# Down projection of a decoder layer: block products over seven instead of eight for 24 of 44 K tiles, in written order

## The chip, the cores and the metric

The kernel runs on one core of a Trainium2 chip. The metric is the device time of one execution in microseconds; the time shown for a kernel is the median of its runs. The profile is one further execution, taken with the hardware profiler on. The work uses TensorE (matmuls into PSUM), VectorE and ScalarE (elementwise), GpSimd (here mostly as the issuer of accumulating DMAs) and SyncE (the issuer of the other DMAs).

## What is computed

One post-norm layer with 512 tokens and width 2048. The change touches only the last stage, `ffn = act @ w_down`, and the residual that is added to it:

```
mix = jnp.einsum('bsm,md->bsd', jnp.concatenate([rg_out, at_out], axis=-1), w_out[i])
x = _layernorm(DEEPNORM_ALPHA * x + mix, ln_mix_g[i], ln_mix_b[i])           # x1
hu = _causal_dwconv(jnp.einsum('bsd,df->bsf', x, w_up[i]), ffn_conv_w[i], ffn_conv_b[i])
g, u = jnp.split(hu, 2, axis=-1)
ffn = jnp.einsum('bsf,fd->bsd', jax.nn.gelu(g) * u, w_down[i])                # 512 x 5632 @ 5632 x 2048
x = _layernorm(DEEPNORM_ALPHA * x + ffn, ln_ffn_g[i], ln_ffn_b[i])
```

All data is float32. The hidden width is 5632 = 44 tiles of 128; the output is 4 token tiles of 128 by 4 column blocks of 512.

## The kernel before, in words

**Numbers in two parts.** Every float32 operand of a matmul is split into a high part (a ScalarE copy to float32r, L113) and a low part (a VectorE subtraction, L114). `split` (L109) does both. A product is three matmuls, high times high, high times low and low times high (`mm3`, L117): each loads a 128x128 block of one operand and streams 512 columns of the other.

**The stages.** Input projections, the recurrent and attention heads, the output projection and its norm come first. Then the up projection: four hidden tiles are made plainly, and the other 40 by `class Pair` (L797 to L909). A pair makes the gate and the up tile of one hidden tile as one 2x2x2 block product with seven products, in the order of `PRODUCTS` (L70). The weight sums that this needs are made by accumulating DMAs that GpSimd issues (`onto`, L807) and by VectorE (L830, L841); each of the seven weights is then split whole, 128x1024 (L816), two steps ahead of its product. The pairs are written out by hand in steps (`step`, L914), one product a step, under `tc.manual_schedule()` (L965): there every engine and every DMA queue executes in written order. The activation of each pair is stored to a DRAM buffer `hidd` (L909).

**The down projection** (L978 to L1014) stands outside the manual schedule, so the scheduler of the language orders it. It goes in chunks of 12, 12, 16 and 4 K tiles (`CHUNKS`, L29). For each of the first three chunks and each column block, four PSUM banks (one for each token tile) take the products of all K tiles of the chunk, and VectorE adds the banks to `acc` (L1007). `acc` is made in the first chunk: x1 without its gain is loaded from the DRAM buffer `x1d` into it (L991), and two VectorE operations apply gain, shift and the residual factor ALPHA (L992, L993). The weights come through `Weights` (L157): six raw buffers of 128x1024 (`RAW_UP`, L54), three pairs of split buffers (`W_BUFS`, L55). The hidden tiles are loaded back and split by `ready` (L958).

**The last chunk** (L1018 to L1036) goes token tile by token tile, with weights that were split beforehand (`keep`), and each token tile is normalized and stored while the next is multiplied. It is the same in both kernels.

Buffers that the change shares: 56 tiles of 128x512 (`A_BUFS`), 12 temporary ones (`T_BUFS`), 8 PSUM banks.

Of the kernel before, what the change touches and what calls it, by code (L numbers as in the profile page):

```python
# [74 lines left out]
def f32(ap):  # L75
    return ap.bitcast(F32)
# [3 lines left out]
def trunk_kernel(  # L80
    ctx, tc, xT, x_tok, w_qkg, w_v, gate_w, w_out, w_up0, w_up, w_down, ln1, ln2, consts, out
):
    nc = tc.nc
# [119 lines left out]
    W = Weights()  # L203
# [717 lines left out]
    j = 0  # L921
# [21 lines left out]
        activate(i, pss)  # L943


    CH = CHUNKS[-1]
    wsrc = iter([w_down[n] for n in range(2 * FT)])
    for c, n in enumerate(CHUNKS[:-1]):
        for u in range(NF * n // 2):
            W.push([next(wsrc)])  # L950

    wlast = [(w, True) for w in wsrc]
    for u in range(len(wlast)):
        W.srcs.insert(len(W.srcs) - 2 * u, wlast[-1 - u])
    keep, gb = [], [[], []]
    hid = {}

    def ready(upto):  # L958
        for i in range(len(hid), min(upto, FT)):
            t = t_tile(F32, "hid")  # L960
            nc.sync.dma_start(t, hidd[i])
            hid[i] = split(t)

    last = NP * len(pairs)
    with tc.manual_schedule():  # L965
        for k in range(last):
            step(k, "early", 1, 8)
            step(k, "late", 7, 16)
            step(k, "before", -6, 5)
            step(k, "product", 0, NP)  # L970
            ready({last - 5: 4, last - 3: 12, last - 2: 16}.get(k, 0))
            if k == last - 4:
                W.load()
    for k in range(last, last + 9):
        step(k, "early", 1, 8)
        step(k, "late", 7, 16)

    acc = {}  # L978
    at = 0
    for c, n in enumerate(CHUNKS[:-1]):  # L980
        ready(at + n)
        for fb in range(NF):
            ps = [bank() for _ in range(QB)]
            if c == 0:

                g1, b1 = [t_tile(F32, "gb1") for _ in range(2)]
                for z, row in ((g1, ln1[0]), (b1, ln1[1])):
                    nc.sync.dma_start(z, row[fb * S : (fb + 1) * S].partition_broadcast(P))
# [5 lines left out]
            for u in range(n // 2):  # L994
                parts = W.take()
                for i in range(2):
                    kk = 2 * u + i
                    for tt in range(QB):
                        hs = [z[:, tt * P : (tt + 1) * P] for z in hid[at + kk]]
                        mm3(ps[tt], hs, parts[i], kk == 0, kk == n - 1)  # L1000
                    if fb == NF - 1 and kk:
                        ready(at + n + kk)
                if c == len(CHUNKS) - 2 and fb == NF - 1 and u >= n // 2 - len(wlast):
                    keep.append(W.take())
            for tt in range(QB):
                y = acc[tt, fb]
                nc.vector.tensor_tensor(y, y, ps[tt], ALU.add)  # L1007
            if c == len(CHUNKS) - 2 and fb < 2:
                for b in range(NF):
                    gb[fb].append(t_tile(F32, "gb"))  # L1010
                    nc.sync.dma_start(
                        gb[fb][b], ln2[fb, b * S : (b + 1) * S].partition_broadcast(P)
                    )
        at += n  # L1014


    ready(FT)
    for tt in range(QB):  # L1018
        tok = slice(tt * P, (tt + 1) * P)
        ns = RowNorm()  # L1020
# [23 lines left out]
def _layout(inputs):  # L1044
# [42 lines left out]
    a["w_down"] = rows(g["w_down"][0], CHUNKS)  # L1087
# [42 lines left out]
```

## Time and profile before

| | |
|---|---|
| median of 3 runs | 2056.37 us (2056.30 to 2056.94) |
| the profiled execution | 2058.12 us, its span in the trace 2055.9 us |
| TensorE busy (matmul) | 2040.5 us, 99% of the span |
| VectorE, ScalarE busy | 1369.0 us (67%), 1039.2 us (51%) |
| GpSimd busy | 108.8 us (5%) |
| pairs of the up projection | about 785 us to 1574 us |
| down projection, last chunk included | from 1562.7 us to the end |

A busy share is over the whole span; the stages differ, so the stage that the change touches is read by itself. A matmul's recorded duration (0.39 us) is not its cost, since matmuls are pipelined: the distance from one start to the next is. The same holds, more weakly, for VectorE and ScalarE, whose consecutive instructions overlap by some hundredths of a microsecond. "Step" means one product's time on TensorE.

### The profile page before, as it was taken

The page shows a single profiled execution, that of the slowest core. Times are in us where ns is not written, and L with a number is a line of the kernel's source. Part 1 is how long each engine was busy: PE and PEld are TensorE (multiplying, and loading weights), DVE is VectorE, ACT ScalarE, POOL GpSimd, SP SyncE. Part 2 cuts the span into 40 slices and gives each one's busy share as a digit, 9 for nine tenths or more (in the row PEclk, how much of TensorE's full clock was granted, in tenths as well). Part 3 has the DMA queues.
Part 4 walks back from the last instruction along what each step waited for, and adds up shares of the span by engine and source line. Part 5 has one row for each costly group of instructions (what it writes and reads, how often), then busy time and mean ns, then how long its engine had stood idle before and what let it go on. Part 6 is the DMA issues. An engine that isn't in the chain of part 4 may idle for free.

```text
span 2055.9 us, 27746 instructions
## 1 busy us (share of the span) xinstructions
PE 2040.5 (99%) x10535; PEld 1747.2 (85%) x10535; DVE 1369.0 (67%) x2148; ACT 1039.2 (51%) x1652; POOL 108.8 (5%) x161
## 2 busy tenths in 40 slices
PE   9999999999999999999999999999999999999997
PEld 7888888888888999888888888888888888888886
DVE  6566645767334677888888888888889643333346
ACT  4475735667223865656556556566565232222232
POOL 1000000010000100100100000001000000000000
PEclk9999999999999999999999999999999999999999
DMA  6322222222533434667667667666678743242322
GB/s 222 98 72 94 77 92 88 88 82 97 175 108 113 154 96 130 176 163 193 171 165 188 173 171 180 169 184 172 168 193 273 264 145 112 93 143 93 113 82 82
DMA packets 93156, 290.52 MB, mean 141 GB/s; under 512 B 10336, under 2 KB 10336, under 8 KB 93024
## 3 DMA queue, kind: packets, MB, share of 16 engines
q1 hardware_dynamic: 81504, 246.81, 35.9%
q0 software_dynamic: 11520, 41.95, 12.1%
q8 instruction: 83, 1.36, 0.3%
q14 instruction: 49, 0.40, 0.1%
HBM read 268.80 MB, written 19.92 MB: 140 GB/s over the span
## 4 chain that ended last, share of the span: by engine, by line
PE 94%; ACT 3%; DVE 1%; issue 0%; DMA 0%; SPq 0%; DVEq 0%
PE ps L120 55%; PE ps L134 37%; PE ps L364 1%; ACT gt L473 0%; PE ps L365 0%; ACT s L376 0%; PE ps L394 0%; PE ps L672 0%; ACT a L479 0%; DMA hid<-hidd 0%; ACT L491 0%; ACT L479 0%; ACT L473 0%; ACT L376 0%; DVE hh L495 0%
## 5 line engine op out<-in xcount | busy, mean ns | idle before, releaser
L114 DVE TENSOR_TENSOR wlo<-raw,whi 128x512 fp32r<-128x512 f32 (+1 forms) x672 | 599.4, 910 | 421.1 <-ACT whi L113 419.8
L113 ACT ACTIVATE whi<-raw 128x512 fp32r<-128x512 f32 (+1 forms) x672 | 523.0, 802 | 470.7 <-PE ps L120 415.4
L120 PE MATMUL ps<-wlo,hi 128*128 128x512 f32 x992 | 386.9, 390 | 0.6 <-DVE wlo L114 0.6
L120 PE MATMUL ps<-whi,hi 128*128 128x512 f32 x992 | 386.6, 390 | 0.6 <-ACT hi L113 0.6
L120 PE MATMUL ps<-whi,lo 128*128 128x512 f32 x992 | 386.5, 390 | 0.0
L134 PE MATMUL ps<-hl,whi 128*128 128x512 f32 x1280 | 320.5, 392 | 0.0
L134 PEld LDWEIGHTS ps<-hl,whi 128*128 128x128 f32 x1280 | 230.2, 189 | 41.1
L134 PE MATMUL ps<-x,whi 128*128 128x512 f32 x960 | 237.1, 389 | 0.0
L120 PEld LDWEIGHTS ps<-whi,hi 128*128 128x128 f32 x992 | 186.7, 188 | 40.3 <-ACT hi L113 1.3
L120 PEld LDWEIGHTS ps<-wlo,hi 128*128 128x128 f32 x992 | 186.7, 188 | 39.7 <-DVE wlo L114 1.0
L120 PEld LDWEIGHTS ps<-whi,lo 128*128 128x128 f32 x992 | 186.7, 188 | 38.6
L134 PEld LDWEIGHTS ps<-x,whi 128*128 128x128 f32 x960 | 180.2, 188 | 37.3
L120 PE MATMUL ps<-hi,whi 128*128 128x512 f32 x512 | 201.9, 394 | 0.0
L120 PE MATMUL ps<-hi,wlo 128*128 128x512 f32 x512 | 200.5, 392 | 1.1 <-DVE wlo L114 1.1
L120 PE MATMUL ps<-lo,whi 128*128 128x512 f32 x512 | 199.9, 390 | 0.0
L134 PE MATMUL ps<-hl,wlo 128*128 128x256 f32 x1280 | 172.9, 283 | 0.0
L134 PEld LDWEIGHTS ps<-hl,wlo 128*128 128x128 f32 x1280 | 164.6, 192 | 3.5 <-ACT cu L881 0.4
L134 PEld LDWEIGHTS ps<-x,wlo 128*128 128x128 f32 x960 | 131.0, 190 | 9.3
L134 PE MATMUL ps<-x,wlo 128*128 128x256 f32 x960 | 133.9, 282 | 0.0
L120 PEld LDWEIGHTS ps<-hi,wlo 128*128 128x128 f32 x512 | 96.1, 188 | 22.7 <-DVE wlo L114 2.4
L120 PEld LDWEIGHTS ps<-lo,whi 128*128 128x128 f32 x512 | 96.3, 188 | 18.5
L120 PEld LDWEIGHTS ps<-hi,whi 128*128 128x128 f32 x512 | 96.2, 188 | 18.3
(187 smaller groups left out, 2231.2 us busy)
## 6 DMA issues: line engine op xcount, KB each, us to landing
raw<-in_w_up SPq DMA_DIRECT2D x176, 512.0 KB, 5.1
raw<-in_w_down SPq DMA_DIRECT2D x88, 512.0 KB, 3.6
raw<-in_w_up POOLq DMA_DIRECT2D x80, 512.0 KB, 6.6
raw<-in_w_qkg SPq DMA_DIRECT2D x64, 512.0 KB, 3.6
raw<-in_w_out SPq DMA_DIRECT2D x32, 512.0 KB, 3.6
hidd<-cv SPq DMA_DIRECT2D x44, 256.0 KB, 3.9
hid<-hidd SPq DMA_DIRECT2D x44, 256.0 KB, 5.2
raw<-in_w_v SPq DMA_DIRECT2D x15, 512.0 KB, 4.4
```

The costliest lines, as they stand in the source:

```text
L113: nc.scalar.activation(hi, src, AF.Copy)
L114: nc.vector.tensor_tensor(lo, src, f32(hi), ALU.subtract)
L120: nc.tensor.matmul(ps, a, b, start=first and n == 0, stop=last and n == 2, skip_group_check=onto)
L134: nc.tensor.matmul(o, a, b, start=not onto and k == 0, stop=k == len(steps) - 1, skip_group_check=onto)
L364: nc.tensor.matmul(ps[:, :L], qs, k[c][:, :L], start=True, stop=False)
```

## The change

The down projection is written out in steps under the manual schedule, with the pairs. `plan` collects actions for a step, and `run` issues them in the order loads, adds from the banks, weight splits (`CUT`), other VectorE and ScalarE work (`SUM`), matmuls.

- The first chunk is 4 K tiles, done plainly (`end_chunk`, 16 steps); the last is 4 as before.
- Between them stand three chunks of 12 K tiles. Eight of the twelve go through block products: tokens in two halves, K in two groups of four, columns in two blocks (`j` and `2 + j`). For each chunk there are two such blocks (`mixed_block`, 22 steps each). A block has seven products instead of eight; the other four K tiles of the chunk are multiplied plainly, half of them straight into the banks of the block products (`plain_lo`), half into banks of their own (`plain_hi`).
- The sums of weights: two accumulating DMAs for each half of the K group (`onto`), two VectorE additions (`s2`, `s4`).
- The sums of hidden blocks (`hid_forms`): three splits of 256 columns, four VectorE additions or subtractions and four more splits for each of four pairs of hidden tiles. Those of the first chunk are made beside `end_chunk`, those of the next chunk beside the second block of the chunk before.
- The residual of x1 is made in place in `x1d` beside the pairs: load, scale (step residue 5 of a pair), shift (7 steps later), store (2 steps after that), 16 tiles, one for every two pairs. `acc` is then only loaded.
- The host lays `w_down` out by column block and pair of K tiles.

```diff
-CHUNKS = [12, 12, 16, 4]
+ENDS = 4
+MIXED, PAIRS, REST = 3, 4, 4
...
+    LOAD, ADD, CUT, SUM, PE = range(5)
...
+    def run(k):
+        for _, fn, args in sorted(todo.pop(k, []), key=lambda z: z[0]):
+            fn(*args)
...
+    def end_chunk(at, k0):
...
+        for fb in range(NF):
+            for u in range(ENDS // 2):
+                k = k0 + 4 * fb + 2 * u
+                plan(max(k - 8, k0 - 6 + 2 * fb + u), LOAD, weights, z, (fb, u), fb, at + 2 * u)
+                plan(k - 2, CUT, cut, w, (fb, u), z, (fb, u))
+                plan(k, PE, product, fb, u)
...
+    def mixed_block(at, j, k0):
...
+        def onto(name, g, n, u):
+            nc.gpsimd.dma_start(
+                z[name, u], w_down[2 * g + j, (at + n * PAIRS) // 2 + u], accum_op=ALU.add
+            )
+        def s2(u):
+            z["s2", u] = W.raw()
+            nc.vector.tensor_tensor(z["s2", u], z["s1", u], z["r11", u], ALU.add)
+        def s4(u):
+            nc.vector.tensor_tensor(z["s2", u], z["s2", u], z["r12", u], ALU.add)
+        def product(name, u):
+            to, new = {"p1": ("x", 1), "p5": ("y", 1), "p2": ("z", 1), "p3": ("y", 0)}.get(name, ("x", 0))
...
+            for i in range(2):
+                f = sides(form2[name, at + 2 * u + i])
+                for t in range(2):
+                    hs = [q[:, t * P : (t + 1) * P] for q in f]
+                    mm3(b[to][t], hs, parts(i), bool(new) and u + i == 0, u + i == 2, not new)
...
+        for u in range(2):
+            for k, fn, args in (
+                (-8, raw, ("s1", 1, 0, u)), (-8, onto, ("s1", 1, 1, u)), (-6, raw, ("r11", 0, 0, u)),
+                (0 + u, onto, ("r11", 1, 0, u)), (1, raw, ("r12", 0, 1, u)),
+                (8, raw, ("r22", 1, 1, u)),
+            ):
+                plan(k0 + k + u, LOAD, fn, *args)
+            plan(k0 + 6 + u, LOAD, weights, z, ("q1", u), lo, rest + 2 * u)
+            plan(k0 + 10 + u, LOAD, weights, z, ("q2", u), hi, rest + 2 * u)
+            for k, name, src in (
+                (-2, "p1", "r11"), (0, "p5", "s1"), (2, "p6", "s2"), (4, "p2", "r12"), (6, "p7", "r11"),
+                (8, "p3", "s2"), (14, "p4", "r22"), (16, "q2", "q2"),
+            ):
+                plan(k0 + k + u, CUT, cut, w, (name, u), z, (src, u))
+            plan(k0 + 10 + 2 * u, CUT, cut, w, ("q1", u), z, ("q1", u))
+            plan(k0 - 1 + 2 * u, SUM, s2, u)
+            plan(k0 + 5 + 2 * u, SUM, s4, u)
+            for k, name in zip((0, 2, 4, 6, 8, 10, 16), PRODUCTS):
+                plan(k0 + k + u, PE, product, name, u)
+            plan(k0 + 12 + 2 * u, PE, plain_lo, u)
+            plan(k0 + 18 + u, PE, plain_hi, "c", ta, u)
+            plan(k0 + 20 + u, PE, plain_hi, "d", tb, u)
+        for k, bank_, tts, fb, op in (
+            (2, "x", ta, lo, ALU.add), (4, "y", tb, hi, ALU.subtract), (6, "x", tb, lo, ALU.add),
+            (10, "x", tb, hi, ALU.subtract), (16, "z", ta, lo, ALU.add), (16, "y", tb, lo, ALU.add),
+            (18, "x", ta, hi, ALU.subtract), (20, "c", ta, hi, ALU.add), (22, "d", tb, hi, ALU.add),
+        ):
+            plan(k0 + k, ADD, added, bank_, tts, fb, op)
...
+    for n in range(QB * NF):
+        k = NP * (2 + 2 * n) + 5 - last
+        plan(k - 5, LOAD, load_z, zs, n)
+        plan(k, SUM, scale_z, zs, n)
+        plan(k + NP, SUM, shift_z, zs, n)
+        plan(k + NP + 2, LOAD, store_z, zs, n)
...
+        for k in range(last, last + END + 1):
+            step(k, "early", 1, 8)
+            step(k, "late", 7, 16)
+            run(k - last)
...
-                for tt in range(QB):
-                    y = acc[tt, fb] = a_tile(F32, "acc")
-                    nc.sync.dma_start(y, x1d[tt][:, fb * S : (fb + 1) * S])
-                    nc.vector.scalar_tensor_tensor(y, y, ALPHA, g1, ALU.mult, ALU.mult)
-                    nc.vector.scalar_tensor_tensor(y, b1, ALPHA, y, ALU.mult, ALU.add)
```

## Rows read from the trace of the kernel before

**Rows 1.** The page, parts 1 and 2: busy time by engine, granted clock by slice.
```profile
PE 2040.5 (99%) x10535; PEld 1747.2 (85%) x10535; DVE 1369.0 (67%) x2148; ACT 1039.2 (51%) x1652; POOL 108.8 (5%) x161
...
PEclk9999999999999999999999999999999999999999
```

**Rows 2.** The page, part 4: the chain that ended last, by line.
```profile
PE ps L120 55%; PE ps L134 37%; PE ps L364 1%; ACT gt L473 0%; PE ps L365 0%; ACT s L376 0%; PE ps L394 0%; PE ps L672 0%; ACT a L479 0%; DMA hid<-hidd 0%; ACT L491 0%; ACT L479 0%; ACT L473 0%; ACT L376 0%; DVE hh L495 0%
```

**Rows 3.** The chain in order of time, from 1540 us: start, length, what.
```profile
1574.05 471.53 PE ps L120 x2080
...
2045.61 0.69 DVE acc L585
```

**Rows 4.** Timeline of TensorE where the pairs end: start, length, line, count.
```profile
1562.69 1.09 PE L120 MATMUL ps<-whi,hi 128*128 128x512 f32 x4
1564.38 0.50 PE L120 MATMUL ps<-wlo,hi 128*128 128x512 f32 x1 [0.60 <-DVE wlo L114]
```

**Rows 5.** Stretches: length; busy PE, PEld, DVE, ACT, POOL (instructions); PEclk, DMA, GB/s.
```profile
1100.00:1200.00 100.00, 100.00 (x576) 88.30 (x576) 86.23 (x98) 60.40 (x78) 8.63 (x10) 1.00 0.68 178
...
1750.00:1800.00 50.00, 50.00 (x222) 41.40 (x222) 17.75 (x27) 11.03 (x19) 0.00 (x0) 1.00 0.31 101
```

**Rows 6.** Waits of all engines, 800 to 1550 us: total, times, longest.
```profile
DVE wlo L114 <- ACT whi L113: 87.1, 116, 2.6
...
ACT whi L113 <- PE ps L134: 10.3, 38, 0.3
```

**Rows 7.** Timeline of TensorE in the pairs, two places.
```profile
1314.84 2.00 PE L134 MATMUL ps<-hl,whi 128*128 128x512 f32 x8
...
1544.16 2.00 PE L134 MATMUL ps<-hl,whi 128*128 128x512 f32 x8
1546.00 1.98 PE L134 MATMUL ps<-x,whi 128*128 128x512 f32 x8
1547.81 1.11 PE L134 MATMUL ps<-x,wlo 128*128 128x256 f32 x8
1548.76 2.00 PE L134 MATMUL ps<-hl,whi 128*128 128x512 f32 x8
```

**Rows 8.** Timeline of VectorE in the pairs.
```profile
1309.43 1.22 DVE L830 TENSOR_TENSOR raw<-raw 128x1024 f32<-128x1024 f32 x1
1310.57 0.68 DVE L883 TENSOR_TENSOR cg<-cg,ps 128x512 f32<-128x512 f32 x1
1311.17 0.68 DVE L884 TENSOR_TENSOR cu<-cu,p 128x512 f32<-128x512 f32 x1
1311.77 1.22 DVE L114 TENSOR_TENSOR wlo<-raw,whi 128x1024 fp32r<-128x1024 f32 x1
```

**Rows 9.** Timeline of VectorE, 256-column work ahead of the pairs.
```profile
772.31 0.42 DVE L762 TENSOR_TENSOR t<-t,x1f 128x256 f32<-128x256 f32 x1
772.65 0.42 DVE L761 TENSOR_TENSOR t<-x1f 128x256 f32<-128x256 f32 x1
```

**Rows 10.** Weight splits on ScalarE by form, whole span: busy, mean ns.
```profile
L113 ACT ACTIVATE whi<-raw 128x1024 fp32r<-128x1024 f32 x280 | 294.6, 1052 | 15.2 <-PE ps L134 10.3 <-PE ps L120 4.2 <-DMA raw<-in_w_up 0.4
```

**Rows 11.** DMA issues, 800 to 1550 us: count, KB each, median us to landing.
```profile
raw<-in_w_up SPq DMA_DIRECT2D x151, 512.0 KB, 5.2
raw<-in_w_up POOLq DMA_DIRECT2D x77, 512.0 KB, 6.0
```

**Rows 12.** The accumulating DMAs of L810, 800 to 1550 us: time to landing.
```profile
DMA to landing us min/median/max: 5.5/6.0/9.9
```

**Rows 13.** Timeline of VectorE as the down projection begins.
```profile
1581.38 0.68 DVE L993 SCALAR_TENSOR_TENSOR acc<-gb,acc 128x512 f32<-128x512 f32 x1
1581.98 1.28 DVE L992 SCALAR_TENSOR_TENSOR acc<-acc,gb 128x512 f32<-128x512 f32 x2
```

**Rows 14.** Waits of SyncE's DMA queue, 800 to 1550 us: total, times, longest.
```profile
SPq L909 <- DVE cv L907: 337.1, 38, 8.9
```

**Rows 15.** Timeline of SyncE's DMA issues in the pairs.
```profile
1313.62 0.33 SPq L909 DMA_DIRECT2D hidd<-cv  x1
```

More of the change, by code (lines that the diff above doesn't have):

```diff
@@ L943, in trunk_kernel @@
         activate(i, pss)
[L946 to L954, printed above, removed]
-    keep, gb = [], [[], []]
[L956 to L962, printed above, removed]
@@ new lines, in split_hid, with add_to, adds, plain @@
+    def split_hid(z, i):
+        hid[i] = split(z.pop(i))
+    def add_to(y, ps, op):
+        nc.vector.tensor_tensor(y, y, ps, op)
+    def adds(k, tts, fb, pss, op=ALU.add):
+        for n, tt in enumerate(tts):
+            plan(k, ADD, lambda tt=tt, n=n: add_to(acc[tt, fb], pss[n], op))
+    def plain(pss, tts, parts, at, first, last, onto=False):
+        for i in range(2):
+            for n, tt in enumerate(tts):
+                hs = [z[:, tt * P : (tt + 1) * P] for z in hid[at + i]]
+                mm3(pss[n], hs, parts(i), first and i == 0, last and i == 1, onto)
@@ new lines, in cut, with side_by, product @@
+    def cut(w, name, z, src):
+        w[name] = split(z[src], *W.pair())
+    def side_by(w, name):
+        return lambda i: [z[:, i * S : (i + 1) * S] for z in w[name]]
+    def end_chunk(at, k0):
+        z, w, pss = {}, {}, {}
+        def product(fb, u):
+            if u == 0:
+                pss[fb] = [bank() for _ in range(QB)]
+                for tt in range(QB):
+                    adds(k0 + 4 * fb + 4, [tt], fb, pss[fb][tt : tt + 1])
+            plain(pss[fb], range(QB), side_by(w, (fb, u)), at + 2 * u, u == 0, u == ENDS // 2 - 1)
+        for fb in range(NF):
[4 more added lines that the diff above has]
+                plan(k, PE, product, fb, u)
@@ new lines, in plan_forms, with raw, added, plain_lo @@
+    def plan_forms(at, ks):
+        for p in range(PAIRS):
+            load, *stages = hid_forms(at, p)
+            plan(ks[p][0] - 5, LOAD, load)
+            for k, fn in zip(ks[p], stages):
+                plan(k, SUM, fn)
+    BLOCK = 22
+    def mixed_block(at, j, k0):
+        z, w, b = {}, {}, {}
+        lo, hi = j, 2 + j
+        ta, tb = (0, 1), (2, 3)
+        rest = at + 2 * PAIRS
+        def raw(name, g, n, u):
+            weights(z, (name, u), 2 * g + j, at + n * PAIRS + 2 * u)
+        def onto(name, g, n, u):
[9 more added lines that the diff above has]
+            to, new = {"p1": ("x", 1), "p5": ("y", 1), "p2": ("z", 1), "p3": ("y", 0)}.get(name, ("x", 0))
+            if new and u == 0:
+                b[to] = [bank(), bank()]
+            parts = side_by(w, (name, u))
+            for i in range(2):
+                f = sides(form2[name, at + 2 * u + i])
+                for t in range(2):
+                    hs = [q[:, t * P : (t + 1) * P] for q in f]
+                    mm3(b[to][t], hs, parts(i), bool(new) and u + i == 0, u + i == 2, not new)
+        def added(bank_, tts, fb, op):
+            for n, tt in enumerate(tts):
+                add_to(acc[tt, fb], b[bank_][n], op)
+        def plain_lo(u):
+            plain(b["z"] + b["y"], ta + tb, side_by(w, ("q1", u)), rest + 2 * u, False, u == 1, True)
+        def plain_hi(name, tts, u):
+            if u == 0:
+                b[name] = [bank(), bank()]
+            plain(b[name], tts, side_by(w, ("q2", u)), rest + 2 * u, u == 0, u == 1)
+        for u in range(2):
[26 more added lines that the diff above has]
+            plan(k0 + k, ADD, added, bank_, tts, fb, op)
@@ new lines, in trunk_kernel, with load_acc @@
+    raws = {}
+    for i in range(ENDS):
+        plan(-9 + i // 2, LOAD, load_hid, raws, i)
+        plan(-5 + i // 2, CUT, split_hid, raws, i)
+    def load_acc(fb):
+        for tt in range(QB):
+            acc[tt, fb] = a_tile(F32, "acc")
+            nc.sync.dma_start(acc[tt, fb], x1d[tt][:, fb * S : (fb + 1) * S])
+    for fb in range(NF):
+        plan(-3 + fb, LOAD, load_acc, fb)
+    end_chunk(0, 0)
+    START = 4 * NF
+    plan_forms(ENDS, [[1, 2, 3], [5, 6, 7], [9, 10, 11], [12, 13, 14]])
@@ new lines, in trunk_kernel, with load_gb, split_keep @@
+    END = k1 + BLOCK
+    def load_gb(n, fb):
+        gb[n].append(t_tile(F32, "gb"))
+        nc.sync.dma_start(gb[n][fb], ln2[n, fb * S : (fb + 1) * S].partition_broadcast(P))
+    def split_keep(z, n):
+        keep.append([split(z[n][:, i * S : (i + 1) * S]) for i in range(2)])
+    for n in range(2):
+        for fb in range(NF):
+            plan(k1 + 2 + 2 * fb + n, LOAD, load_gb, n, fb)
+    kept = {}
+    for n, (k, kl) in enumerate(((11, 8), (13, 9), (15, 12), (17, 13), (19, 14), (20, 15), (22, 16), (22, 17))):
+        plan(k1 + kl, LOAD, weights, kept, n, n // 2, FT - ENDS + 2 * (n % 2))
+        plan(k1 + k, SUM, split_keep, kept, n)
@@ new lines, in trunk_kernel, with load_z @@
+    for n, k in enumerate((12, 14, 18, 19)):
+        plan(k1 + k - 4, LOAD, load_hid, raws, FT - ENDS + n)
+        plan(k1 + k, SUM, split_hid, raws, FT - ENDS + n)
+    last = NP * len(pairs)
+    def load_z(z, n):
+        fb, tt = divmod(n, QB)
+        if tt == 0:
+            z["g"], z["b"] = [t_tile(F32, "gb1") for _ in range(2)]
+            for m, row in ((z["g"], ln1[0]), (z["b"], ln1[1])):
+                nc.sync.dma_start(m, row[fb * S : (fb + 1) * S].partition_broadcast(P))
+        z[n] = t_tile(F32, "z")
+        nc.sync.dma_start(z[n], x1d[tt][:, fb * S : (fb + 1) * S])
@@ L970, in trunk_kernel @@
             step(k, "product", 0, NP)
[L971 to L988, printed above, removed]
-                for tt in range(QB):
-                    y = acc[tt, fb] = a_tile(F32, "acc")
-                    nc.sync.dma_start(y, x1d[tt][:, fb * S : (fb + 1) * S])
-                    nc.vector.scalar_tensor_tensor(y, y, ALPHA, g1, ALU.mult, ALU.mult)
-                    nc.vector.scalar_tensor_tensor(y, b1, ALPHA, y, ALU.mult, ALU.add)
[L994 to L1017, printed above, removed]
+            run(k - last)
+        for k in range(last, last + END + 1):
+            step(k, "early", 1, 8)
+            step(k, "late", 7, 16)
+            run(k - last)
+    at = FT - ENDS
     for tt in range(QB):
```

65 lines of the change are left out of this document (64 added, 1 removed).

## The prediction

> **What bounds the kernel now.** I read the busy shares first: TensorE is busy 99% of the span at full granted clock in every slice [rows 1]. A busy share alone proves little where matmuls are pipelined, so the chain that ended last comes next: 55% and 37% of the span are TensorE at the two matmul helpers (L120, L134), and no other entry is above 1% [rows 2]. Then the stage of the change: from 1574.05 us on, 2080 matmuls take 471.53 us in one unbroken piece [rows 3]; that is 0.2267 us each, end to end, at granted clock 1.00 [rows 5]. So the down projection is paid by the matmul, and in that stretch VectorE is busy 17.75 of 50 us and ScalarE 11.03. After the last matmul there are 10.3 us of norm and store (2045.61 to 2055.9) [rows 3], which both kernels have.
>
> The model for the changed stage is the pairs, which already work as the changed stage will: seven products, splits two steps ahead, written order. There TensorE is busy 100.00 of 100 us beside a VectorE that is busy 86.23 [rows 5], and among the waits there is none of TensorE; what they hold of the splits is VectorE waiting for ScalarE's copies and ScalarE waiting for TensorE to give back a split buffer [rows 6].
>
> **What is removed.** One product of a block goes over four K tiles (two weight buffers of two) and two token tiles, three matmuls each: 4 x 2 x 3 = 24 matmuls of 512 columns. Eight become seven, in 3 chunks x 2 blocks = 6 blocks: 6 x 24 = 144 matmuls less, 2112 to 1968. At 0.2267 us this is **32.6 us**. The pitch of the new products could differ, since their stationary blocks come from tiles with both parts side by side. The nearest row is the pairs: eight 512-column matmuls take 1546.00 - 1544.16 = 1.84 us (0.230) or 1547.81 - 1546.00 = 1.81 us (0.226) [rows 7]. For the 6 x 7 x 24 = 1008 matmuls of the products that bounds the pitch's part at -1 to +3 us; I take 0, as the shapes are those of L120.
>
> **The seam between pairs and down projection.** Four matmuls start at 1562.69 and the fifth only at 1564.38, after VectorE's low part [rows 4]: 1564.38 - (1562.69 + 4 x 0.2267) = 0.8 us lost. In the changed kernel the first product's weights are split two steps ahead and its hidden tiles four to five steps ahead, so this could go. But new seams come (pairs to plain chunk, plain chunk to blocks, block to block), so I take 0 gain, bounds -0.8 to +3 us.
>
> **What is added on VectorE.** Prices are start-to-start: 1.14 us for 1024 columns (1309.43 to 1310.57), 0.60 for 512 [rows 8], 0.34 for 256 [rows 9]. A step of the down projection is 12 matmuls, 2.72 us; a block is 22 steps, 59.9 us.
> - A block: 18 weight splits and 4 weight sums of 1024, 18 bank additions of 512: 22 x 1.14 + 18 x 0.60 = 36 us. With the four plain hidden tiles of the chunk 38 us, 64%.
> - A block beside which the next chunk's hidden sums are made (two such): 44 operations of 256 columns more, 36 + 44 x 0.34 = 51 us, 85%.
> - The plain chunk, 16 steps or 43.6 us: nine weight splits and one sum in it, 12 bank additions, 44 operations of 256, the end of the last pair (eight operations of 512): 10 x 1.14 + 20 x 0.60 + 44 x 0.34 = 38.4 us, 88%.
>
> No stretch is above what the pairs show beside an unbroken TensorE. Step by step, with 2.72 us of VectorE per step and what is left over carried on, the backlog is highest at the steps with four bank additions: 1.5 us in the chunk's fifth step, 1.8 in its thirteenth, 0.8 in step 16 of each block; it is gone two or three steps later each time. A weight split is written two steps, 5.44 us, ahead of its product. At a four-addition step the way to its end is: the last matmul's end 0.4, four additions 2.4, the low part 1.14, together 3.9 us (4.6 in the fifth step, where a convolution stands ahead). So it lies beside other work: cost 0. Should that cover fail, what is queued behind the waiting addition is the weight split, and TensorE waits for it; this is the first rival.
>
> ScalarE gets the same splits at 1.05 us [rows 10]; with half of that for a copy of 256, surely too much, 18 x 1.05 + 28 x 0.53 = 34 of 59.9 us in the fullest block. Off the path.
>
> **What is added in DMA.** A block issues 12 plain loads of 512 KB from SyncE and 4 accumulating ones from GpSimd in 59.9 us; three pairs (58 us) issue 12 and 6 and a few stores. So the queues see no more than they do now. Landing is 5.2 and 6.0 us [rows 11], 9.9 at worst for the accumulating ones [rows 12]. The shortest way is `r12`: its buffer is given back by the split of `p5` in the step before, it is cut three steps later (8.2 us): 3 us of cover beyond 5.2, and its product is two steps behind. The accumulation onto `r11` may start after the sums of steps -1 and 1 and is cut at 6 and 7, five steps or 13.6 us. Cost 0.
>
> Here a rule speaks against the change. The rows show that an accumulating 512 KB DMA from GpSimd lands in a median of 6.0 us and a plain one from SyncE in 5.2 us, while VectorE is busy 86% of the time [rows 5, 11]. The Trainium skill, page "SBUF — State Buffer", section "SBUF: two separate sides", says that a DMA from the GpSimd queue gets its descriptors written over a port that VectorE can hold in some modes, so that it looks blocked by VectorE; its section "Who interferes with whom" excepts two-input operations from that in part. By the rule the accumulations would land late and the sum would lose what the third rival says; by the rows they lose 0.8 us that is covered.
>
> **What is moved.** Residual: 32 VectorE operations of 512 columns (0.60 each [rows 13], 19 us) leave the down projection's start and go beside the pairs, one for each pair, with 16 loads, 16 stores (new: 4 MB) and 8 broadcast loads on SyncE's queue. A pair is seven steps of some 2.77 us (1548.76 - 1546.00 [rows 7]), 19.4 us; VectorE's busy time in it goes from 16.7 to 17.3 us. In the written order the operation stands behind the residue-5 split and sum and ahead of the two additions of the next step and the split of `p5`. That split ends at 1311.77 + 1.22 = 1312.99 [rows 8], and its product starts at 1314.84 [rows 7], with its low part used half a product later. 0.6 us more is covered by 1.85. On SyncE's queue the store and the next load stand just ahead of the `hidd` store, at which the queue waits up to 8.9 us for VectorE, 337 us in 38 waits [rows 14]; the store waits for a shift that VectorE does two steps before the product that `hidd` waits for. So they fall into that wait: cost 0. If the cover went, `r21`, the next load, would be late; that is the slower rival. What the down projection's start gains from the removal is nothing on TensorE's path.
>
> **Sum.** Span 2055.9 - 32.6 = 2023.3 us. The median of the runs stands 0.5 us above the span of the profiled execution (2056.37 to 2055.9; its own time is 2058.12), so 2023.7: forecast **2024 us**, 1.6% less.
>
> **Rivals.**
> - *VectorE paces the four-addition steps.* There are ten: four for the plain chunk, six in the blocks. If none of the backlog is hidden, each costs 0.8 to 1.8 us: 8 to 18 us, 2032 to 2042. For: VectorE is in the written order and stands waiting for banks with splits behind it. Against: the pairs, 86% busy, without a wait. Chance 0.15.
> - *Smaller pauses* at seams and a 0.230 pitch, up to +5 us: inside the forecast's own range.
> - *The accumulating DMAs come late.* It decides from a landing above 13.6 us, against 6.0 now and 9.9 at worst. At 20 us each block would lose some 5 us, 6 x 5 = 30: 2054, no change. Chance 0.03.
> - *It doesn't do what it says:* the seven products give no fewer TensorE cycles, because each matmul of the block costs 8/7 (0.259 us). The rows for 512 columns go from 0.226 to 0.230 [rows 7]. That would be 2056. Chance 0.01.
> - *Slower: the pairs get longer.* Place: the queue of SyncE and VectorE in each of 40 pairs. If scaling waits for its load or the `z` store holds up `r21`, the split of `p5` is late and TensorE waits in every other pair or more. It decides from 32.6 / 40 = 0.82 us per pair: then the gain is eaten. With nothing hidden, VectorE's 0.60 us and one DMA issue of 0.33 us [rows 15] per pair make 40 x 0.93 = 37 us: 2061. Against it: 1.85 us of cover on VectorE, up to 8.9 us on the queue. Chance 0.05.
>
> **How the numbers follow.** Forecast with its small pauses (2021.9 to 2029) 0.76, first rival 0.15, late DMAs 0.03, no saving 0.01, longer pairs 0.05. The bottom of the range is the sum with the seam's 0.8 us gained and 1 us of pitch: 2021.9. The top takes in half of the first rival: 2036; about 0.83 lies between. A difference of 0.2%, 4 us, is about the least that a measurement of this kernel can tell from no change. Faster by more: forecast, first rival, 0.91. Within: late DMAs and no saving, 0.04. Slower: 0.05.
>
> **What would show it.** Down projection: 1968 matmuls at 0.227 us, ending some 32 us earlier; no wait of TensorE for VectorE above a microsecond; VectorE busy about 85% in the second blocks of chunks one and two, about 64% in the first blocks. Pairs: 19.4 us each as before, VectorE at about 89%. Accumulating DMAs: a median near 6 us in both stages. Wrong: gaps of TensorE every 60 us at step 16 of a block (first rival), gaps before `p7` (late DMAs), a longer period of the pairs (slower rival).

## The result and the profile after

| | before | after |
|---|---|---|
| median of 3 runs | 2056.37 us (2056.30 to 2056.94) | 2024.95 us (2024.00 to 2027.03) |
| ratio of the times | | 0.9848, 95% interval 0.9826 to 0.9871 |
| the profiled execution, its span | 2058.12, 2055.9 us | 2024.95, 2023.2 us |

The time falls by 1.5%, 31.4 us between the medians; 2024 was forecast. The page of after, parts 1 and 4, answers [rows 1, 2]:

```profile
PE 2006.7 (99%) x10391; PEld 1719.2 (85%) x10391; DVE 1502.4 (74%) x2312; ACT 1082.9 (54%) x1668; POOL 129.4 (6%) x185
...
PE ps L122 54%; PE ps L136 36%; DMA raw<-in_w_up 2%; DVE wlo L116 1%; PE ps L366 1%; ACT gt L475 1%; PE ps L367 0%; ACT s L378 0%; PE ps L396 0%; PE ps L674 0%; ACT a L481 0%; ACT L493 0%; ACT L481 0%; ACT L475 0%; ACT L378 0%
```

TensorE still is the bound, with 144 matmuls less (10535 to 10391). VectorE has 133 us more to do and stays off the chain of the down projection. One entry is new: 2% of the chain is DMA of the pairs' weights (`in_w_up`), in a stage whose matmuls the change doesn't touch.

The chain in order of time, after, from 1540 us on (start, length, what), answers [rows 3]:

```profile
1539.84 26.93 PE ps L136 x152
1566.77 446.09 PE ps L122 x1968
2012.86 0.02 issue
2012.89 0.69 DVE acc L587
```

From the pairs' end to the end of TensorE's work there is one piece: 1968 matmuls in 446.09 us, 0.2267 us each, without a wait. To cut the two spans into the same parts, the first product of the pairs is needed, from TensorE's timeline of before and of after:

```profile
785.73 2.00 PE L134 MATMUL ps<-x,whi 128*128 128x512 f32 x8
```

```profile
783.83 2.00 PE L136 MATMUL ps<-x,whi 128*128 128x512 f32 x8
```

In before, 16 matmuls of the last pair (3.01 us in its chain) stand among the first ones of the down projection, so its pairs take 1562.69 - 785.73 + 3.01 = 779.97 us [rows 4] and the rest up to 2045.59 is seam and down projection.

| part | before | after | difference |
|---|---|---|---|
| ahead of the pairs | 785.73 | 783.83 | -1.90 |
| pairs | 779.97 | 782.94 | +2.97 |
| seam and down projection | 479.89 | 446.09 | -33.80 |
| last norm and store | 10.31 | 10.34 | +0.03 |
| span | 2055.9 | 2023.2 | -32.7 |

The first line is no effect of the change: the same program, profiled again (below), has its pairs begin at 786.2 us. The other two are: 144 x 0.2267 = 32.64 us for the matmuls and 1.16 us for the seam are won, and some 3 us are lost in the pairs. The forecast put both of the small ones at 0; together they are +1.8 us, and the first line happens to take that back.

VectorE by stretches of after, in the order plain chunk, then the six blocks (columns as in [rows 5]):

```profile
1567.00:1610.60 43.60, 43.60 (x194) 36.08 (x194) 40.50 (x77) 21.59 (x42) 2.59 (x3) 1.00 0.72 237
1610.60:1670.50 59.90, 59.90 (x266) 49.61 (x265) 38.63 (x43) 21.30 (x23) 2.59 (x3) 1.00 0.56 154
1670.50:1730.40 59.90, 59.90 (x266) 49.61 (x265) 52.26 (x85) 28.28 (x47) 3.45 (x4) 1.00 0.63 180
...
1910.00:1969.90 59.90, 59.90 (x266) 49.60 (x265) 45.17 (x56) 27.37 (x36) 1.72 (x2) 1.00 0.66 202
```

The sum said 38.4, 38, 51 us for the first three and gave no figure for the last; they are 40.50, 38.63, 52.26 and 45.17. The first stretch is not quite the sum's: it takes in, from 1608.53 us on, most of the four additions that end the chunk, which the sum leaves out. The 74 operations that the sum counts are by themselves 38.97 us busy (1566.46 to 1608.53). TensorE is busy in the whole of each stretch. The waits of all engines in the pairs of after, 800 to 1560 us, answer [rows 6]:

```profile
POOL raw L812 <- DMA raw<-in_w_up: 239.3, 28, 11.6
...
ACT whi L115 <- DMA raw<-in_w_up: 41.3, 31, 4.5
...
DVE raw L832 <- DMA raw<-in_w_up: 10.7, 11, 3.2
...
PEld ps L136 <- ACT cv L786: 2.2, 2, 1.4
PE ps L136 <- DVE wlo L116: 1.8, 2, 1.2
```

There the 3 us begin. `r21` is a raw weight buffer of a pair: SyncE loads one block of weights into it, and GpSimd's DMA adds a second one. GpSimd waits for the load of `r21` 239 us in all; in before this row had 36.6 us. The row by itself is no loss: all waits of GpSimd together are about the same (702 us before, 705 after), and what changed is which of the things that it waits for comes last. The loss shows in the rows behind it: ScalarE and VectorE wait for what GpSimd added (41 and 11 us; 0.4 and none before), and at two places TensorE waits for VectorE.

### The profile page after: what moved, and what is told of

It reads as the page before. It is cut to its first block, busy times and chain, and to the rows that moved or that the text cites. A ratio compares the mean times of both kernels' runs of the same rounds, so it can differ in the third digit from the quotient of the medians.

```text
span 2023.2 us, 27822 instructions
## 1 busy us (share of the span) xinstructions
PE 2006.7 (99%) x10391; PEld 1719.2 (85%) x10391; DVE 1502.4 (74%) x2312; ACT 1082.9 (54%) x1668; POOL 129.4 (6%) x185
## 4 chain that ended last, share of the span: by engine, by line
PE 92%; ACT 3%; DVE 2%; DMA 2%; issue 1%; SPq 0%; DVEq 0%; POOLq 0%
PE ps L122 54%; PE ps L136 36%; DMA raw<-in_w_up 2%; DVE wlo L116 1%; PE ps L366 1%; ACT gt L475 1%; PE ps L367 0%; ACT s L378 0%; PE ps L396 0%; PE ps L674 0%; ACT a L481 0%; ACT L493 0%; ACT L481 0%; ACT L475 0%; ACT L378 0%
## 5 line engine op out<-in xcount | busy, mean ns | idle before, releaser
L116 DVE TENSOR_TENSOR wlo<-raw,whi 128x1024 fp32r<-128x1024 f32 (+1 forms) x628 | 637.1, 1024 | 310.0 <-ACT whi L115 304.8
L115 ACT ACTIVATE whi<-raw 128x1024 fp32r<-128x1024 f32 (+1 forms) x628 | 553.6, 895 | 451.7 <-PE ps L122 329.0
L122 PE MATMUL ps<-whi,hi 128*128 128x512 f32 x608 | 237.1, 390 | 0.2 <-ACT hi L115 0.2
L122 PE MATMUL ps<-wlo,hi 128*128 128x512 f32 x608 | 236.8, 389 | 0.0
L122 PE MATMUL ps<-whi,lo 128*128 128x512 f32 x608 | 236.5, 389 | 0.0
L122 PE MATMUL ps<-whi,hl 128*128 128x512 f32 x672 | 208.8, 389 | 0.0
L122 PEld LDWEIGHTS ps<-whi,hl 128*128 128x128 f32 x672 | 126.1, 188 | 26.2
L122 PEld LDWEIGHTS ps<-whi,lo 128*128 128x128 f32 x608 | 114.1, 188 | 23.8 <-DVE lo L116 0.2
L122 PEld LDWEIGHTS ps<-wlo,hi 128*128 128x128 f32 x608 | 114.3, 188 | 23.5
L122 PE MATMUL ps<-wlo,hl 128*128 128x512 f32 x336 | 130.7, 389 | 0.0
```

What stands on the lines that cost most here:

```text
L122: nc.tensor.matmul(ps, a, b, start=first and n == 0, stop=last and n == 2, skip_group_check=onto)
```

## The experiments

All times are medians of their runs. They were taken in three groups (e1 to e4, e5 to e8, e9 to e12), each beside before, which stood at 2056.67, 2056.23 and 2058.15 us; so 2 us between kernels of different groups is not told by the times, and the parts of the profiles decide. "Pairs" is the time from the first product of the pairs to the first matmul of the unbroken piece of the down projection, in the profile of each kernel; without any wait it is 780.0 us. For before and e2 the 16 matmuls that stand later are counted in, as above, and their down projection holds the seam.

| kernel | time | pairs | down projection | GpSimd's wait for `r21` |
|---|---|---|---|---|
| before | 2056.37 | 780.0 | 479.89 | 37 |
| changed kernel | 2024.95 | 782.9 | 446.09 | 239 |
| e11: the same, again | 2025.66 | 781.3 | 446.09 | 239 |
| e1: residual back in the plain chunk | 2042.73 | 779.8 | 463.6 | 39 |
| e2: before with the residual moved | 2059.07 | 781.3 | 479.81 | 236 |
| e3: written order, all chunks plain | 2056.89 | 781.3 | 478.73 | 236 |
| e4: one middle chunk of seven products | 2047.75 | 783.4 | 467.85 | 237 |
| e5: moved DMAs without VectorE's part | 2024.03 | 780.0 | 446.09 | 218 |
| e6: VectorE's part without the DMAs | 2022.49 | 780.0 | 446.09 | 39 |
| e7, e12: residual loaded one step earlier | 2024.23, 2022.88 | 780.0, 780.0 | 446.09, 446.09 | 241, 243 |
| e8: VectorE +0.6 us in every step | 2034.47 | 782.3 | 454.3 | 241 |
| e9: VectorE +0.6 us in every second step | 2025.13 | 781.2 | 446.14 | 241 |
| e10: residual in the blocks | 2022.92 | 780.0 | 446.09 | 38 |

### Is it the count of matmuls?

The written order stays, and the middle chunks go plainly, as `end_chunk` does it, with 12 K tiles:

```diff
-    for c in range(MIXED):
...
-        for j in range(2):
-            mixed_block(at, j, k0 + j * BLOCK)
+    KINDS = "PPP"
...
+            for n in range(12):
+                plan(k0 - 18 + n, LOAD, load_hid, raws, at + n)
+                plan(k0 - 14 + n, SUM, split_hid, raws, at + n)
+            end_chunk(at, k0, 12)
+            k0 += 48
```

> The changed kernel with all three middle chunks of 12 K tiles done plainly in the same written order and with the same residual beside the pairs: 2112 matmuls again. Theory: only the count of matmuls pays, so 2025 + 32.6 = 2057 to 2058 us, with 0.2267 us per matmul. Rival: a part of the gain is from the written order or from the seam, then 2040 to 2050 us.

Measured: 2056.89 us, ratio to before 0.9999 (0.9990 to 1.0009). With `KINDS = "MPP"`:

> As the kernel with all chunks plain in written order, but the first of the three middle chunks through the seven products: 48 matmuls less than eight products everywhere. Theory: 10.9 us less than that kernel, 2046 to 2047 us, a third of the gain. Rival: the first block product costs more than it saves by waits at its start, so less than 5 us.

Measured: 2047.75 us, ratio 0.9956 (0.9942 to 0.9971). The chains, all plain and then one chunk of seven products:

```profile
1566.80 478.73 PE ps L122 x2112
```

```profile
1569.44 467.85 PE ps L122 x2064
```

478.73 / 2112 = 467.85 / 2064 = 446.09 / 1968 = 0.2267 us. 48 matmuls less are 478.73 - 467.85 = 10.88 us, 144 less are 478.73 - 446.09 = 32.64 us: the saving is the count times the pitch, with nothing lost at the blocks' seams. The difference of the medians (9.1 us for the first chunk) is less exact than that, since e4's profile has 2.1 us more in the pairs. The written order by itself is worth nothing in the time: it wins the seam, 479.89 - 478.73 = 1.16 us, and the residual's move that stands in the same kernel loses 1.4 us in the pairs.

### How much cover has VectorE in the blocks?

```diff
+    def extra():
+        t = t_tile(F32, "more")
+        nc.vector.tensor_tensor(t, cst[:, :S], cst[:, :S], ALU.add)
+
+    for k in range(START, END, 1):
+        plan(k, SUM, extra)
```

> The changed kernel with one more VectorE operation of 512 columns (0.60 us) in every step of the six blocks, its result unused. By the sum the two blocks with hidden sums go from 51 to 64 of 59.9 us and must be paced by VectorE, the others go to 51 (55 in the last) and must not: 2025 + 2 x (4 to 6) = 2033 to 2037 us, the waits in the second blocks of the first two middle chunks alone. Rival 1 (waits between the engines limit earlier than busy time): light blocks lose too, 2045 us or more. Rival 2: the cover is larger, below 2028 us.

Measured: 2034.47 us, 9.5 more than the changed kernel. Its stretches:

```profile
1610.00:1670.00 60.00, 60.00 (x266) 49.68 (x265) 50.76 (x64) 21.41 (x23) 2.59 (x3) 1.00 0.55 154
1670.00:1733.00 63.00, 60.56 (x260) 49.54 (x259) 62.73 (x106) 28.04 (x46) 3.45 (x4) 0.97 0.61 171
1733.00:1793.00 60.00, 60.00 (x266) 49.70 (x265) 53.07 (x68) 21.21 (x22) 3.45 (x4) 1.00 0.58 154
1793.00:1858.00 65.00, 62.54 (x276) 51.14 (x275) 64.72 (x107) 29.34 (x47) 3.45 (x4) 1.00 0.60 166
```

Only the two blocks with hidden sums lose: there VectorE is busy 62.73 of 63 and 64.72 of 65 us and sets the pace. The first blocks, at 50.76 and 53.07 of 60, lose nothing. The down projection is 8.2 us longer (454.3), and the sum had 4 us of excess in each of the two blocks. With a step of 2 in the loop:

> The changed kernel with one more VectorE operation of 512 columns in every second step of the six blocks, its result unused (half the dose of the kernel with one in every step, which took 2034.5 us). By the sum the blocks with hidden sums go from 51 to 57.6 of 59.9 us and still fit: 2025 to 2027 us. Rival: the price is per operation, not by a threshold, then half of 9.5 us: 2029 to 2030 us.

Measured: 2025.13 us (the changed kernel beside it 2025.66), the down projection 446.14 us. The stretch of the first block with hidden sums; in the second VectorE is busy for 57.68 us too:

```profile
1670.00:1730.00 60.00, 60.00 (x266) 49.70 (x265) 57.68 (x95) 28.27 (x46) 3.46 (x4) 1.00 0.64 180
```

VectorE is busy 57.68 of 60 us, 96%, beside a TensorE that never waits. So the price is a threshold, somewhere between 96% and all of the block's own length, and not a price per operation. The changed kernel stands 7 us under that length.

### What does the move of the residual cost, and where?

The kernel before with the move alone (the functions `load_z` to `store_z` and their plan put into its loop of pairs, L992 and L993 taken out):

> The kernel before with the residual alone moved beside the pairs; the down projection as before, eight products in the scheduler's order. Theory: nothing gained in the down projection, whose TensorE had no wait for it, and 2 to 3 us lost in the pairs: 2058 to 2060 us, GpSimd's wait for its loads in the pairs at some 240 us. Rival, of the prediction: the move is hidden, 2056 us, or it frees the seam, 2055 us.

Measured: 2059.07 us, ratio 1.0012 (1.0002 to 1.0021). The move alone makes the kernel slower, by 2.4 us, its pairs are 1.4 us longer in the profile, and GpSimd's wait is 236 us.

Back in the plain chunk, where the changed kernel would otherwise have it:

```diff
+    def residual(fb, tt):
+        y, (g1, b1) = acc[tt, fb], gbs[fb]
+        nc.vector.scalar_tensor_tensor(y, y, ALPHA, g1, ALU.mult, ALU.mult)
+        nc.vector.scalar_tensor_tensor(y, b1, ALPHA, y, ALU.mult, ALU.add)
...
+        for tt in range(QB):
+            plan(4 * fb + tt, SUM, residual, fb, tt)
```

> The changed kernel with the residual's 32 VectorE operations, its loads of gain and shift back in the plain chunk (two operations a step there), nothing of it beside the pairs. Theory: the move costs TensorE some 3 us in the pairs through DMA order, and pays for itself because VectorE has no room for it in the plain chunk: 38.4 + 19.2 = 57.6 us of VectorE in 43.6 us of steps, so TensorE falls 8 to 12 us behind there, while the pairs get 3 us shorter (GpSimd's wait for the loads in the pairs back from 239 us to about 40): 2030 to 2034 us. Rival: the plain chunk's cover is larger than the sum says and the move was needless: 2022 us, no wait of TensorE in the plain chunk.

Measured: 2042.73 us, 17.8 more than the changed kernel, where 5 to 9 more were expected. The plain chunk's stretch:

```profile
1564.00:1630.00 66.00, 55.23 (x219) 43.57 (x217) 62.32 (x111) 24.39 (x44) 2.59 (x3) 0.92 0.58 186
```

The kind was right: VectorE paces, and the move out of this chunk is what makes the chunk fit. The size was not: the down projection is 17.5 us longer (463.6). The operations of the sum take VectorE 62.9 us, from 1564.11 to 1627.01 (the stretch shown holds four additions more): 2.9 us of that are two waits, which the sum didn't have, and the other 60.0 stand against its 57.6. TensorE waits four times (5.1, 0.6, 2.7 and 2.9 us), each time for a weight split that stands on VectorE behind the four additions from the banks, and its granted clock falls to 0.92. The price of the operations has its reason in VectorE's timeline, in those that read the result of the one just before:

```profile
1591.45 0.69 DVE L1157 SCALAR_TENSOR_TENSOR acc<-gb,acc 128x512 f32<-128x512 f32 x1
1592.06 0.42 DVE L1032 TENSOR_TENSOR t<-hid 128x256 f32<-128x256 f32 x1
1592.52 0.42 DVE L1033 TENSOR_TENSOR t<-t,hid 128x256 f32<-128x256 f32 x1
1592.97 0.42 DVE L1034 TENSOR_TENSOR t<-t,hid 128x256 f32<-128x256 f32 x1
1593.32 0.42 DVE L1035 TENSOR_TENSOR t<-hid 128x256 f32<-128x256 f32 x1
```

L1033 needs L1032's result and starts 0.46 us after it, L1034 needs L1033's and starts 0.45 after it; L1035 needs neither and starts 0.35 after. The sum had 0.34 for all. The pair L1156 and L1157 of the residual is of that sort too (0.71 instead of 0.60, shown below). There are 8 + 16 such operations in the chunk, so an estimate from these rows is 24 x 0.11 = 2.6 us, which is about the 2.4 that the sum was short.

Which part of the move costs? The DMAs without VectorE's part (the residual then lacks gain, shift and factor):

```diff
-        plan(k, SUM, scale_z, zs, n)
-        plan(k + NP, SUM, shift_z, zs, n)
```

> The changed kernel with the residual's loads, broadcasts and stores beside the pairs but without its 32 VectorE operations (the residual then lacks gain, shift and factor). Theory (the DMAs cost the 3 us in the pairs: the load of r21 is issued right behind the z load and lands late): GpSimd's wait for its loads in the pairs stays near 200 us, the time at 2023 to 2026 us. Rival (VectorE's added 0.6 us per pair): waits as before the change, about 40 us, and 2022 us.

Measured: 2024.03 us (2022.40 to 2025.31), pairs 780.0 us, no wait of TensorE in them. By the time alone this can't be told from the changed kernel; the pairs in the profile tell it. VectorE's part without the DMAs:

```diff
-        plan(k - 5, LOAD, load_z, zs, n)
...
-        plan(k + NP + 2, LOAD, store_z, zs, n)
```

> The changed kernel with the 32 VectorE operations beside the pairs on data that lies in SBUF, and none of the residual's loads, broadcasts and stores there (the residual lacks gain, shift and factor). Theory: GpSimd's wait for its loads in the pairs back to about 40 us, no wait of TensorE there, pairs 3 us shorter, 2021 to 2022.5 us. Rival (VectorE): 2024 to 2025 us as the changed kernel.

Measured: 2022.49 us, pairs 780.0 us, GpSimd's wait 39 us. So neither part alone makes TensorE wait: my theory for e5 was half wrong, since GpSimd does wait there (218 us), but nobody behind it. What needs both is an order: the store of a tile must wait for VectorE's shift, and it stands on SyncE's queue ahead of the next tile's loads. SyncE's issues in the changed kernel, where a new column block begins:

```profile
1134.79 0.33 SPq L1206 DMA_DIRECT2D x1d<-z  x1
1135.17 0.92 SPq L1194 DMA_DIRECT2D gb<-in_ln  x2
1136.13 0.43 SPq L1196 DMA_DIRECT2D z<-x1d  x1
1137.73 0.33 SPq L911 DMA_DIRECT2D hidd<-cv  x1
1138.15 9.52 SPq L807 DMA_DIRECT2D raw<-in_w_up  x4
```

The shift (L1202) starts on VectorE at 1134.08; until it is done the store is held, and with it gain, shift row and tile, 0.75 MB. They are issued at 1135 to 1136.6, just ahead of the load of `r21` at 1138.15. In e5, where the store waits for nothing, the same three loads go out at 1129.9 to 1131.4, while the `hidd` store still waits until 1138.3:

```profile
1129.44 0.42 SPq L1206 DMA_DIRECT2D x1d<-z  x1
1129.92 0.93 SPq L1194 DMA_DIRECT2D gb<-in_ln  x2
1130.89 0.49 SPq L1196 DMA_DIRECT2D z<-x1d  x1
```

They land at most 6.6 us after their issue in that run, so their transfer is over before `r21`'s begins. GpSimd, ScalarE, VectorE and TensorE after that load, in the changed kernel:

```profile
1146.89 0.86 POOL L812 DMA_DIRECT2D raw<-in_w_up  x1 [11.34 <-DMA raw<-in_w_up]
```

```profile
1155.80 1.06 ACT L115 ACTIVATE whi<-raw 128x1024 fp32r<-128x1024 f32 x1 [4.54 <-DMA raw<-in_w_up]
```

```profile
1155.72 1.23 DVE L832 TENSOR_TENSOR raw<-raw 128x1024 f32<-128x1024 f32 x1 [3.20 <-DMA raw<-in_w_up]
```

```profile
1162.36 1.19 PE L136 MATMUL ps<-hl,wlo 128*128 128x256 f32 x8 [1.21 <-DVE wlo L116]
```

`r21` lands 8.7 us after its issue (1138.15 to 1146.89); in the same pair of before it takes 5.2 us, of e5 5.9. The accumulation lands 8.9 us later, the split of `p5` on ScalarE is 4.5 us late, the sum L832 stands 3.2 us at the head of VectorE's queue with the splits behind it, and two splits later TensorE waits 1.2 us.

This doesn't happen in every pair. TensorE's only other wait for VectorE in the pairs of this profile is:

```profile
1004.63 1.19 PE L136 MATMUL ps<-hl,wlo 128*128 128x256 f32 x8 [0.63 <-DVE wlo L116]
```

It comes 26 us behind the loads that begin the second column block (978.36); the wait at 1162.36 comes 27 us behind those of the third (1135.17). The seven profiles with the residual in this place have 14 such waits in the pairs: seven behind the loads of the second column block, one in each profile, five behind the third's or the fourth's, and two elsewhere (1360.3 in e4, 1357.2 in e8). None comes behind the first column block's loads, ahead of which no store stands.

If it is the order, the loads need only stand elsewhere, one step earlier, ahead of the load of `r22`:

```diff
-        plan(k - 5, LOAD, load_z, zs, n)
+        plan(k - 6, LOAD, load_z, zs, n)
```

> The changed kernel with the residual's loads planned one step earlier, so that they stand ahead of the load of r22 (which has room) and not between it and the load of r21. Theory: the load of r21 lands in time, GpSimd's wait falls towards 100 us or less, TensorE's waits in the pairs go, 2022 to 2023 us. Rival: it is the amount of data, not its place: no change, 2025 us.

Measured: 2024.23 us, by the times alone not to be told from the changed kernel. Its profile had pairs of 780.0 us, the same issues at

```profile
1123.64 0.90 SPq L1194 DMA_DIRECT2D gb<-in_ln  x2
1124.58 0.47 SPq L1196 DMA_DIRECT2D z<-x1d  x1
1127.33 0.33 SPq L807 DMA_DIRECT2D raw<-in_w_up  x1
1134.30 0.33 SPq L1206 DMA_DIRECT2D x1d<-z  x1
1137.23 0.33 SPq L911 DMA_DIRECT2D hidd<-cv  x1
```

and no wait of TensorE; `r21` lands 5.8 us after its issue there. That GpSimd's wait would fall was wrong (241 us): it waits often, but at most 10.1 us and not 11.6, and the rest is covered. So it was run again, beside the changed kernel:

> The changed kernel with the residual's loads one step earlier, once more. Theory (the z store waits for its shift and holds the loads behind it until the load of r21 is due): pairs of 780 us in the profile again, no wait of TensorE in them, and 2 to 3 us less than the changed kernel beside it. Rival: the first look was a lucky one, pairs of 781 to 783 us and no difference.

> The changed kernel as it is, once more, for the same chip and hour as the others of this call. 2024 to 2026 us; pairs of 781 to 783.5 us from their first product to the first matmul of the down projection.

Measured: 2022.88 us (five runs, 2022.67 to 2025.24) against 2025.66 us (five runs, 2025.37 to 2026.21): every run of the one is below every run of the other. Pairs of 780.0 us once more, against 781.3.

### A version that is faster than both

The first block of each middle chunk has 20 us of room on VectorE (e8 used 13 of them at no cost), so the residual can go there, without stores and without the order's trouble:

```diff
+    def add_z(z, n):
+        fb, tt = divmod(n, QB)
+        y = acc[tt, fb]
+        nc.vector.scalar_tensor_tensor(z[n], z[n], ALPHA, z["g", fb], ALU.mult, ALU.mult)
+        nc.vector.scalar_tensor_tensor(y, z["b", fb], ALPHA, y, ALU.mult, ALU.add)
+        nc.vector.tensor_tensor(y, y, z[n], ALU.add)
...
+    for fb, c, ks in ((0, 0, (11, 12, 13, 14)), (1, 0, (15, 17, 18, 19)), (2, 1, (12, 13, 15, 19)), (3, 2, (12, 13, 15, 19))):
```

> The changed kernel with the residual neither beside the pairs nor in the plain chunk, but in the three first blocks of the middle chunks, where VectorE has 20 us of room: 8, 4 and 4 tiles, three operations each (1.8 us); the plain chunk starts the accumulators by copies, half of them on ScalarE. Theory: pairs 780 us as without the move, down projection 446.1 us unbroken, 2021.5 to 2023 us, some 2.5 us less than the changed kernel. Rival: the three more operations or their loads make TensorE wait in the first blocks: 2025 us or more.

Measured: 2022.92 us (five runs, 2022.20 to 2024.46), ratio to before 0.9833 (0.9819 to 0.9847), 2.7 us below the changed kernel beside it. TensorE has no wait from the first pair to the last matmul. The block with eight tiles of the residual has VectorE at 53.14 of 60 us:

```profile
1607.00:1667.00 60.00, 60.00 (x267) 49.67 (x266) 53.14 (x68) 21.94 (x24) 3.46 (x4) 1.00 0.71 206
```

It and e12 are 2.7 and 2.8 us faster than the changed kernel beside them and can't be told from each other.

## Why the prediction was right, step by step

- **The matmuls.** Right to the hundredth: 144 x 0.2267 = 32.64 us, and the pitch of the new products is that of L120. The bound of +3 us for it was not needed. e3 and e4 show that this term is all of the gain but the seam's 1.16 us.
- **The seam.** Taken at 0 with -0.8 as its lower end; it gave -1.16 us (479.89 to 478.73), a little beyond that end. The seams that were feared in its place cost nothing.
- **VectorE in the blocks.** The sums held: 38.97 against 38.4 us, 38.63 against 38, 52.26 against 51. That no stretch would be above what the pairs show was wrong for the plain chunk, already by its own 88% against their 86; with the four additions at its end the stretch is at 93% (40.50 of 43.6 us). The price of 0.34 us for every operation of 256 columns is too low for chained ones, which take 0.45. The cover held all the same: e9 shows that it holds at 96% of a block.
- **The first rival** (the four-addition steps) didn't come: no wait of TensorE in the down projection. e8 and e1 show that its mechanism is real (splits behind waiting additions, TensorE behind the splits), but that it sets in when VectorE's work of a stage nears the stage's length, and not with the backlog of 0.8 to 1.8 us at one step.
- **DMA in the blocks.** 6 us for the accumulating DMAs was too short: their median in the down projection is 7.9 us, 10.5 at most. The decision point of 13.6 was not reached, so the cost of 0 was right.

The rows of the accumulating DMAs in the down projection and in the pairs of the changed kernel, and of e6 in the pairs (count, KB, median to landing):

```profile
raw<-in_w_down POOLq DMA_DIRECT2D x24, 512.0 KB, 7.9
```

```profile
raw<-in_w_up POOLq DMA_DIRECT2D x77, 512.0 KB, 7.6
```

```profile
raw<-in_w_up POOLq DMA_DIRECT2D x77, 512.0 KB, 6.3
```

With VectorE's added work and none of the added DMAs (e6) the landing is 6.3 us; with the DMAs and none of the work (e5) 7.1; with both 7.6. With neither it is 6.0 in before, 6.5 in e10 and 6.9 in e1, so these medians scatter by almost a microsecond. Seven profiles with the added traffic (the changed kernel, e2, e3, e5, e7, e11, e12) lie at 7.0 to 7.6. So what lengthens the landing is the other traffic; VectorE's added work by itself, in e6, leaves it within the scatter. The Trainium skill's rule on descriptors held up by VectorE ("SBUF — State Buffer", "SBUF: two separate sides") isn't seen at work in these runs; they agree with its exception for two-input operations ("Who interferes with whom").

- **The move of the residual.** This is the step that failed: "they fall into that wait: cost 0". It costs 1.2 to 3.4 us in the seven profiles that have it in this place. What was right: VectorE's 0.6 us is covered (e6), the added issues do fall into the wait of the `hidd` store, and `r21` is not issued later (19.5 us after that of the pair before, in before and after). What was missed: the store's own wait holds back the loads behind it, and where these are three, at a new column block, `r21` then lands late (8.7 us after its issue instead of 5.2) because their bytes are on the way. The slower rival had the place (the store, `r21`, the split of `p5`) with the wrong price: 37 us with nothing hidden, against 3.
- **The sum.** By the spans it came out to 0.1 us, 2023.3 against 2023.2, and that is luck: -1.16 (seam) and +2.97 (pairs), both taken at 0, and -1.90 ahead of the pairs, where nothing was changed, add up to -0.1. The median stands 1.25 us above the sum's 2023.7 because the 0.5 us that the sum adds is the distance of before's median from the span of another execution, the profiled one. Within one execution the time is 1.75 us above the span after the change (2024.95, 2023.2) and 2.2 before it (2058.12, 2055.9).
- **The time of the profiled execution.** Its own time was 2058.12, 1.75 above the median. The part ahead of the pairs, which the change doesn't touch, differs by up to 2.4 us between executions of one program (783.83 and 786.2 us for the changed kernel), and the spread of the runs is of that size. A step of 3 us in the pairs therefore shows in the parts of a profile before it shows in a median of three.

## What to carry to other kernels

Where one engine is busy throughout at a steady pitch, price a change there by its count of instructions, and give the others' work stage by stage against the stage's length: here 96% of it cost nothing, and above it about the excess was paid. A DMA that must wait for an engine holds everything behind it on its queue; plan loads that need not wait ahead of it, and ask not only whether the next urgent load is issued in time but whose bytes are in flight when it is. Small terms that were put at 0 are worth an experiment each, since a good total may be luck: they can cancel.

## What the runs showed of the hardware

VectorE operations that read the result of the one just before start about 0.11 us later than independent ones: 0.45 instead of 0.35 us at 256 columns, 0.71 instead of 0.60 at 512 (e1: L1156 and L1157, with the next independent one behind):

```profile
1567.18 0.68 DVE L1156 SCALAR_TENSOR_TENSOR acc<-acc,gb 128x512 f32<-128x512 f32 x1
1567.89 0.69 DVE L1157 SCALAR_TENSOR_TENSOR acc<-gb,acc 128x512 f32<-128x512 f32 x1
1568.50 0.68 DVE L892 TENSOR_TENSOR cu<-cu 128x512 f32<-128x512 f32 x1
```

The chained one starts 0.03 us after the recorded end of the one before it (1567.18 + 0.68 to 1567.89), the independent one 0.08 us ahead of it. The Trainium skill, page "VectorE: DVE Perf Modes", section "The DRAIN you can't avoid", has the same time for eight copies with a semaphore after each as with one after the last. It doesn't say whether one copy reads the other's result, so the rows here, of chained against independent operations, neither bear it out nor speak against it.

In e1 TensorE stood for 5.1 us waiting for a split and then ran at its lower level, 1.2 GHz (granted clock 0.50 from 1586.1 to 1592.0 us):

```profile
1580.58 0.39 PE L122 MATMUL ps<-whi,hi 128*128 128x512 f32 x1
1586.08 0.79 PE L122 MATMUL ps<-wlo,hi 128*128 128x512 f32 x1 [5.11 <-DVE wlo L116]
1586.67 0.63 PE L122 MATMUL ps<-whi,lo 128*128 128x512 f32 x1
1587.10 0.63 PE L122 MATMUL ps<-whi,hi 128*128 128x512 f32 x1
```

Twelve starts are 0.43 us apart instead of 0.227, until 1591.8. After a wait of 2.7 us that ends at 1614.5, six matmuls still start 0.23 to 0.35 us apart, and seven starts from 1616.1 on are 0.43 us apart again (granted clock 0.50 from 1616.0 to 1619.2). After the wait of 2.9 us that ends at 1630.67 there are none. The 19 slow starts are 19 x 0.20 = 3.9 us of TensorE's time. Since VectorE set the pace there (busy 5.80 of the first 5.90 us), the rows don't tell how much of the 17.8 us they added; that was not tried.
